# The o projection by seven products: where the sums of its weights and operands are made, and when its operands are loaded

## The chip, the cores and the metric

The kernel runs on one core of one Trainium2 chip. Its engines work side by side: TensorE (PE in the profile, its weight loads PEld), VectorE (DVE), ScalarE (ACT), GpSimd (POOL) and SyncE (SP), which issues most of the transfers (DMA). Each engine takes its instructions in order, and waits for other engines and for transfers by semaphores. The metric is the time of one execution on the chip in microseconds (us), lower is better. Before the change it is 1758.16 us, the median of three runs (1757.42 to 1760.56).

## What is computed

One layer of a hybrid encoder on 1024 positions and 1024 channels in float32: a norm, a projection into many column groups, a convolution module and a bidirectional gated recurrence side by side, a gated merge of the two, an output projection and a feed-forward part. What the change touches are the lines that follow the recurrence, and the layer norm of the convolution module:

```python
a = jax.nn.glu(glu_in, axis=-1)
a = _dwconv_centred(a, dw_w, dw_b)
a = jax.nn.silu(_layernorm(a, ln_w, ln_b))
a = jnp.einsum("bsc,cd->bsd", a, pw_w)
o = _bi_hgrn2(q, v, z_f, z_b, lb[0], lb[1])
...
bmix = (of * jax.nn.silu(og.astype(jnp.float32))).astype(h.dtype)
bmix = jnp.einsum("bse,ed->bsd", bmix, o_w)                      # the o projection
return jax.nn.sigmoid(g_a) * a + jax.nn.sigmoid(g_b) * bmix      # the merge
...
x = x + h @ w_out
```

## The kernel before

**Precision.** A float32 matrix product is made of three passes in a reduced format: each operand is split into a high part (a cast on ACT) and a low part (a subtraction on DVE or POOL; `split`, L126), and `mm3` (L150 to L152) adds high by high, high by low and low by high.

**Seven products.** Large projections are cut into 2 x 2 blocks and made by seven block products instead of eight. For that, sums of blocks of the weights and sums of blocks of the operand are needed. For the o projection the operand is the recurrence's gated output, kept in DRAM as d_bm[head][half] (eight heads of 128 channels, two halves of 512 positions). Blocks are b11 (heads 0 to 3, half 0), b12 (heads 0 to 3, half 1), b21 (heads 4 to 7, half 0) and b22 (heads 4 to 7, half 1). Products 1, 2 and 3 use blocks as they are, products 4 to 7 use sums: 7 is b22 - b12, 5 and 6 and 4 build on it and on b11 and b21. Each product has four columns of output and four slices k of 128 channels.

**Order.** PE's order is written out in the program. Work that must be done beside it is queued by `later(n, f)`: f runs n steps of the stream of products later, and issues its instructions at that place. The other engines' order is made by the framework's scheduler from there, except that an instruction given to `pin` keeps its place in the program. SP's transfers go in its own order; a transfer that waits holds up those behind it.

**The stages, in order of time.**

- *The convolution's norm* (`conv_norm`, L1107 on; about 375 to 470 us, two halves). DVE subtracts the mean (L1124), ACT squares, DVE adds the squares (L1129, three times), PE sums over partitions into the bank ob (L610), DVE and POOL make the reciprocal root (L614, L583, L584). Between these steps PE works on other products. In the same stretch `o_sums` (L1085) loads blocks of the o weights (L1090), adds them on DVE (L1094, four a time, 32 in all) and stores them in d_os (L1095); its start and its additions are set by O_STEP and O_LATE.
- *The scan* (about 600 to 882 us): eight heads one after another, with a stream of other products between; POOL spreads state rows (L1395, S<-D) and makes the root of each head's norm (L583, L584). `scan_outputs` scales the head's output, transposes it (L1484), multiplies by the gate (L1486) and stores d_bm (L1487). `bm_loads` (L1525) reads half 0 back and splits it as operand of products 1 and 2.
- *The o projection* (882.28 to 998.84 us): 28 products of 12 matmuls each, in the order 1 (four columns), 2 (four), 6 (four), then 7 and 4 by turns, 5 (four), 3 (four). Weights come in 14 groups of two products (`o_load`, tag wr, two buffers). `operands` (L1620 on) reads d_bm back, makes the sums (L1635; slices 0 to 2 on POOL, slice 3 on DVE) and splits them. After a product with a finished block, `merge` (L1588) loads a gate from d_gb, multiplies (L1602, L1604), adds the convolution's part by an accumulating transfer on POOL's queue (L1605) and splits the outcome into pages mg. Product 7's outcome is copied from its bank to xq on ACT (L1689) before product 4 adds on to the same bank.
- *The projection by w_out* (998.84 to 1094.26 us), and beside both of these `weight_sums` (L1709): sums of the next layer part's weights, loaded at L1715, added on DVE at L1724 and stored in d_us at L1725.

Of the kernel before, what the change touches and what calls it, by code (L numbers as in the profile page):

```python
# [24 lines left out]
O_LATE, O_STEP = 5, 4  # L25
# [24 lines left out]
def tile_hybrid_encoder(  # L50
# [418 lines left out]
    cp.tile([P, ALIGN // 4 - 8], F32, name="offset")  # L469
# [87 lines left out]
    d_us = [dp.tile([P, 4, ND // 2 * P], F32, name=f"d_us_{n}") for n in range(3)]  # L557
    d_os = [dp.tile([P, 4, ND // 2 * P], F32, name=f"d_os_{n}") for n in range(ND // 2)]
# [526 lines left out]
    def o_sums(n):  # L1085
# [6 lines left out]
        def add():  # L1092
            for a, b in ((0, 1), (1, 2), (2, 0), (3, 2)):
                pin(V.tensor_tensor(t[:, a], t[:, a], t[:, b], op=ALU.add))  # L1094
            nc.sync.dma_start(d_os[p].rearrange("p q (k e) -> p q k e", e=P)[:, :, ks], t)  # L1095

        later(O_LATE, add)
# [116 lines left out]
    none = hp.tile([P, ALIGN // 2], mybir.dt.bfloat16, name="none")[:, :32]  # L1214
# [224 lines left out]
    def scan_outputs(h, kept, Sf, Sb):  # L1439
# [41 lines left out]
        for half in range(2):  # L1481
# [5 lines left out]
            nc.sync.dma_start(d_bm[h][half], bt)  # L1487
            yield
# [34 lines left out]
    b_o = {i: [None] * NK2 for i in range(1, 8)}  # L1523

    def bm_loads():  # L1525
        for h in range(NH - 1):
            t = page(hp, "A", 8)
            nc.sync.dma_start(t, d_bm[h][0])
            behind = last_turned if h < NH - 2 else last_scaled
            with tc.issue_after(behind[0].ins):  # L1530
                b_o[1 + h // NK2][h % NK2] = split(hx(), hx(), t, V)
# [84 lines left out]
    b_pages = {i: [(mg_page(), mg_page()) for _ in range(NK2)] for i in (4, 5)}  # L1616

    def operand(i, k, t):
        pages = b_pages[i][k] if i in b_pages else (hx(), hx())
        b_o[i][k] = split(*pages, t, V)  # L1620

    def operands(k):
        eng = V if k == NK2 - 1 else G
        b11, b12, b22, b21 = [
            h7_page(d_bm[k + h * NK2][half]) for h, half in ((0, 0), (0, 1), (1, 1), (1, 0))
        ]
        if k == NK2 - 1:
            operand(2, k, b21)
        for i, o, a, b, op in (
            (7, b22, b12, b22, ALU.subtract),  # L1630
# [602 lines left out]
```

## Time and profile before

| what | value |
|---|---|
| time, median of three runs | 1758.16 us (1757.42 to 1760.56) |
| the profiled execution | 1759.66 us, span of its instructions 1757.9 us |
| mean clock granted to PE | 0.983 of full speed |
| PE busy in the norm's windows | 6.55 us of 390 to 400, 5.16 us of 450 to 460 |
| o projection | 116.56 us long, PE busy 84.69, DMA share 0.83 |
| projection by w_out | 95.42 us long, PE busy 90.76, DMA share 0.54 |

The page gives busy times of each engine over the whole span. The view of waits names, for each engine, the instruction that waited and what ended the wait. A window lists, for each engine, its busy time and in brackets its instructions, then the clock granted to PE (1.00 is full), the mean share of the DMA engines and GB/s. A row of the timeline has start and length in us, the engine, the line, the operation, the tiles (out<-in), a count where like instructions follow one another, and in square brackets the idle time before it with what ended it. A row of grouped instructions has after the bar the busy us and the mean ns of one, then idle time.

### The profile page before, as it was taken

To read this page: it belongs to the slowest core of one execution; us is meant where nothing else is said; L and a number is where in the kernel's file an instruction comes from. 1 tells how busy PE (TensorE), PEld (TensorE's weight loads), DVE (VectorE), ACT (ScalarE), POOL (GpSimd) and SP (SyncE) were. 2 spreads that over 40 slices of the span, in tenths; PEclk is the share of its full clock that TensorE was granted. 3 is DMA by queue.
4 is the path that set the end of the run, shared out by engine and by line. 5 is a ranking of instruction groups with operands and counts; after the bars stand their busy time and mean duration, and the time that the engine had idled before them with its cause. 6 is when DMAs were issued, how large, how long until landed. Compare 5 with 4: busy or idle time off the path is not lost. (4 is left out here: it accounts for less than half of the span.)

```text
span 1757.9 us, 30563 instructions
## 1 busy us (share of the span) xinstructions
PE 1696.7 (97%) x11671; PEld 1407.7 (80%) x11671; DVE 1303.5 (74%) x1988; ACT 847.6 (48%) x1592; POOL 278.7 (16%) x315
## 2 busy tenths in 40 slices
PE   9999999999899999999957899999999999999998
PEld 6788888887788888888845678888888888888787
DVE  5888898986678888887575556776777777657865
ACT  7454343334477777776433344543443444442434
POOL 2212222100001111111140100322222212000110
PEclk9999999999899999999979999999999999999999
DMA  6888888866663443437679754676777777683752
GB/s 240 289 210 186 199 196 190 206 215 218 219 229 111 126 143 114 155 104 241 219 231 270 177 172 155 177 168 150 168 174 163 166 178 167 201 265 115 209 104 97
DMA packets 348280, 321.64 MB, mean 183 GB/s; under 512 B 18654, under 2 KB 256358, under 8 KB 348134
## 3 DMA queue, kind: packets, MB, share of 16 engines
q1 hardware_dynamic: 298470, 276.69, 49.0%
q0 software_dynamic: 49664, 43.01, 16.6%
q8 instruction: 91, 1.49, 0.3%
q14 instruction: 55, 0.45, 0.1%
HBM read 212.14 MB, written 89.65 MB: 172 GB/s over the span
## 5 line engine op out<-in xcount | busy, mean ns | idle before, releaser
L150 PE MATMUL mm<-hx,wp 128*128 128x512 f32 x976 | 391.1, 401 | 0.6 <-ACT wp L126 0.6
L152 PE MATMUL mm<-hx,wp 128*128 128x512 f32 x976 | 382.0, 391 | 1.3 <-DVE wp L126 1.3
L151 PE MATMUL mm<-hx,wp 128*128 128x512 f32 x976 | 381.3, 391 | 0.6 <-POOL hx L126 0.6
L126 ACT CAST wp<-wr 128x1024 fp32r<-128x1024 f32 (+2 forms) x152 | 153.2, 1008 | 230.2 <-PE mm L151 164.7
L152 PEld LDWEIGHTS mm<-hx,wp 128*128 128x128 f32 x976 | 183.7, 188 | 42.2 <-DVE wp L126 2.6
L126 DVE TENSOR_TENSOR wp<-wr,wp 128x1024 fp32r<-128x1024 f32 (+2 forms) x150 | 176.9, 1179 | 53.3 <-ACT wp L126 53.0
L150 PEld LDWEIGHTS mm<-hx,wp 128*128 128x128 f32 x976 | 183.9, 188 | 38.2 <-ACT wp L126 1.2
L151 PEld LDWEIGHTS mm<-hx,wp 128*128 128x128 f32 x976 | 184.1, 189 | 36.6 <-POOL hx L126 1.1
L1073 DVE SCALAR_TENSOR_TENSOR acc<-gl,v_b,acc 128x1024 f32<-128x1024 f32 x120 | 153.5, 1281 | 1.7
L150 PE MATMUL tr<-hx,wp 128*128 128x512 f32 x200 | 78.3, 392 | 17.5 <-ACT hx L126 17.5
L442 ACT COPY su<-mm 128x512 f32<-128x512 f32 x82 | 47.8, 583 | 87.1 <-PE mm L152 87.0
L1395 POOL DMA_DIRECT2D S<-D x64 | 36.4, 574 | 281.1 <-ACT jk L1462 125.3
L152 PE MATMUL tr<-hx,wp 128*128 128x512 f32 x200 | 78.2, 391 | 1.6 <-DVE wp L126 1.6
L151 PE MATMUL tr<-hx,wp 128*128 128x512 f32 x200 | 78.2, 391 | 1.3 <-DVE hx L126 1.3
L1218 DVE TENSOR_TENSOR qF<-qF,tb 128x512 f32<-128x512 f32 x96 | 65.7, 684 | 9.5 <-ACT A L1252 8.9
L126 ACT CAST wq<-sw 128x1024 fp32r<-128x1024 f32 x41 | 43.2, 1053 | 59.5 <-PE mm L151 29.8
L1218 DVE TENSOR_TENSOR kG<-kG,tb 128x512 f32<-128x512 f32 x96 | 65.7, 686 | 4.0 <-ACT A L1252 2.3
L1812 DVE SCALAR_TENSOR_TENSOR tm<-gp,v_a,tm 128x512 f32<-128x512 f32 x88 | 66.0, 750 | 3.3 <-ACT tm L1810 1.3
L303 POOL DMA_DIRECT2D sw<-in_ffn_w_up_dram x38 | 49.7, 1484 | 117.5 <-DMA sw<-in_ffn_w_up_dram 79.8
L150 PE MATMUL sc<-hy,wq 128*128 128x512 f32 x164 | 64.4, 393 | 0.0
L151 PE MATMUL sc<-hy,wq 128*128 128x512 f32 x164 | 64.3, 392 | 0.0
L152 PE MATMUL sc<-hy,wq 128*128 128x512 f32 x164 | 64.3, 392 | 0.0
(431 smaller groups left out, 3929.4 us busy)
## 6 DMA issues: line engine op xcount, KB each, us to landing
wr<-in_w_in_dram SPq DMA_DIRECT2D x48, 512.0 KB, 5.7
wr<-in_ffn_w_up_dram SPq DMA_DIRECT2D x22, 512.0 KB, 5.3
sw<-in_w_in_dram SPq DMA_DIRECT2D x38, 256.0 KB, 3.1
d_g<-ft SPq DMA_DIRECT2D x38, 256.0 KB, 2.2
sw<-in_ffn_w_up_dram SPq DMA_DIRECT2D x38, 256.0 KB, 4.2
sw<-in_ffn_w_up_dram POOLq DMA_DIRECT2D x38, 256.0 KB, 6.4
wr<-sw POOLq DMA_DIRECT2D x32, 256.0 KB, 3.2
wr<-wr POOLq DMA_DIRECT2D x32, 256.0 KB, 3.3
```

Source lines behind the costliest of these rows:

```text
L126: parts = A.copy(hi, src), eng.tensor_tensor(lo, src, hi.bitcast(F32), op=ALU.subtract)
L150: T.matmul(acc, whi[:, k, :], ahi, start=first, stop=False, skip_group_check=again)
L151: T.matmul(acc, whi[:, k, :], alo, start=False, stop=False, skip_group_check=again)
L152: T.matmul(acc, wlo[:, k, :], ahi, start=False, stop=last, skip_group_check=again)
L303: G.dma_start(o, a, accum_op=ALU.add)
L442: A.copy(t, acc)
L1073: V.scalar_tensor_tensor(acc, g[:, k : k + S], tap(k), acc, op0=ALU.mult, op1=ALU.add)
L1218: return V.tensor_tensor(o, a, b, op=op)
L1395: G.dma_start(S_t[g : g + 32, :, g : g + 32], D_t[g : g + 32])
L1812: V.scalar_tensor_tensor(c, g[:, o + k : o + k + H], vec("fdw", k * NF + j), c, op0=ALU.mult, op1=ALU.add,)
```

## The change

1. In the norm, the loads of the o weights keep their place within a few steps, but the 32 additions are no longer made five steps after the loads: they are handed back as single closures, and run two a step from the step on which the third addition of squares is out.
2. The operand sums of slices 0 to 2 are made in the scan. `combine(k)` starts after the second half of heads 4, 5 and 6 (k = 0, 1, 2): it loads three blocks of d_bm, and a fourth later, into pages ws (three buffers), has POOL add four times (5, 7, 9 and 17 steps later), and stores each sum in a new place in DRAM, d_bt.
3. In the o stage, operands 6, 7, 4 and 5 of slices 0 to 2 are loaded from d_bt and split, dealt over the stage by `later`; slice 3 is still summed on DVE, also dealt. Loads of operand 3 are dealt in a chain. One half of slice 3 of operand 2 is split straight from the tile that holds it, without a reload. Every third weight group goes to a page sw of another pool, so there are three buffers.
4. The additions of `weight_sums` are pinned to the place where the program issues them.

```diff
-O_LATE, O_STEP = 5, 4
...
+    d_bt = {i: scratch(f"d_bt_{i}", ND // 2) for i in (4, 5, 6, 7)}
...
-        def add():
-            for a, b in ((0, 1), (1, 2), (2, 0), (3, 2)):
-                pin(V.tensor_tensor(t[:, a], t[:, a], t[:, b], op=ALU.add))
-            nc.sync.dma_start(d_os[p].rearrange("p q (k e) -> p q k e", e=P)[:, :, ks], t)
-
-        later(O_LATE, add)
+        def add(a, b):
+            pin(V.tensor_tensor(t[:, a], t[:, a], t[:, b], op=ALU.add))
+            if a == 3:
+                nc.sync.dma_start(d_os[p].rearrange("p q (k e) -> p q k e", e=P)[:, :, ks], t)
+
+        return [lambda a=a, b=b: add(a, b) for a, b in ((0, 1), (1, 2), (2, 0), (3, 2))]
...
     for half in range(2):
+        sums = []
         for n in range(half * ND // 2, half * ND // 2 + ND // 2):
-            later(1 + O_STEP * (n % (ND // 2)), lambda n=n: o_sums(n))
-        for pieces in conv_norm(half):
+            later(6 + 2 * (n % 4), lambda n=n: sums.extend(o_sums(n)))
+        for n, pieces in enumerate(conv_norm(half)):
+            if n == 14:
+                for m in range(16):
+                    later(1 + m // 2, lambda m=m: sums[m]())
             s_pairs.fill(pieces)
...
+            if h == NH - 1 and half == 0:
+                b_o[2][NK2 - 1] = split(*b_pages[2][NK2 - 1], bt, V)
+            if half and NK2 <= h < NH - 1:
+                later(2, lambda: combine(h - NK2))
...
+    def combine(k):
+        def raw(src):
+            t = page(hp, "ws", 3)
+            nc.sync.dma_start(t, src)
+            return t
+
+        def keep(i, o, a, b, op=ALU.subtract):
+            G.tensor_tensor(o, a, b, op=op)
+            nc.sync.dma_start(d_bt[i][k], o)
+
+        b12, b22, b11 = [
+            raw(d_bm[k + h * NK2][half]) for h, half in ((0, 1), (1, 1), (0, 0))
+        ]
+        last = []
+        later(5, lambda: keep(7, b22, b12, b22))
+        later(7, lambda: keep(5, b12, b11, b12))
+        later(9, lambda: keep(6, b11, b22, b11))
+        later(12, lambda: last.append(raw(d_bm[k + NK2][0])))
+        later(17, lambda: keep(4, last[0], b11, last[0], ALU.add))
...
+    for k in range(k3):
+        fetched(0, 3 + k, 6, k, d_bt[6][k])
+    raw3 = [h7_page(d_bm[k3][half]) for half in range(2)]
+    later(3, lambda: raw3.extend(h7_page(d_bm[NH - 1][half]) for half in (1, 0)))
...
+    later(6, last_sums)
+    later(17, lambda: operand(5, k3, raw3[1]))
+    later(18, last_fourth)
+    later(19, lambda: operand(7, k3, raw3[2]))
+    for k in range(k3):
+        fetched(9 + k, 6, 7, k, d_bt[7][k])
+        fetched(17 + k, 4, 4, k, d_bt[4][k])
+        fetched(22 + 2 * k, 5, 5, k, d_bt[5][k])
+
+    def third(k):
+        b_pages.setdefault(3, []).append((hx(), hx()))
+        fetched(0, 5, 3, k, d_bm[k + NK2][1])
 
     for k in range(NK2):
-        operands(k)
-
-    for k in range(NK2):
-        later(28 + 2 * k, lambda k=k: operand(3, k, h7_page(d_bm[k + NK2][1])))
+        later(28 + 2 * k, lambda k=k: third(k))
...
-            o_raws[g] = mp.tile([P, 2 * NK2, P], F32, tag="wr", name=nm("wr"), bufs=2)
+            if g % 3 < 2:
+                o_raws[g] = mp.tile([P, 2 * NK2, P], F32, tag="wr", name=nm("wr"), bufs=2)
+            else:
+                o_raws[g] = fw.tile([P, 2 * NK2, P], F32, tag="sw", name=nm("sw"), bufs=1)
...
-                V.tensor_tensor(t, a, b, op=ALU.add)
+                pin(V.tensor_tensor(t, a, b, op=ALU.add))
```

`fetched(at, late, i, k, src)` loads a page, at steps from now, and splits it late steps after that; `last_sums` and `last_fourth` are the four additions of slice 3 on DVE.

The first place is DVE in the second half of the norm, before the change. os are the o weights and their sums, tm the sum of squares, sw and wr weights of other products.

```order
L1094 TENSOR_TENSOR os_4135<-os_4135 128x256 x2
L1124 SCALAR_TENSOR_TENSOR cx_4017<-ob_4161,cx_4017 128x512 x2
L1129 TENSOR_TENSOR tm_4171<-tm_4171,tm_4191 128x512
L836 TENSOR_TENSOR ev_4252<-tr_4177,su_4207 128x512
L1129 TENSOR_TENSOR tm_4171<-tm_4171,tm_4205 128x512
L126 TENSOR_TENSOR wp_4234<-wr_4225,wp_4233 128x1024
L1094 TENSOR_TENSOR os_4185<-os_4185 128x256 x3
L299 TENSOR_TENSOR sw_4227<-sw_4227,sw_4230 128x1024
L1094 TENSOR_TENSOR os_4185<-os_4185 128x256
L299 TENSOR_TENSOR wr_4225<-wr_4225,sw_4227 128x512
L1129 TENSOR_TENSOR tm_4171<-tm_4171,tm_4216 128x512
```

The same place on DVE in the changed kernel (its lines are shifted by a few: L1093 is L1094 above, L298 is L299, L125 is L126).

```order
L125 TENSOR_TENSOR wp_4071<-wr_4050,wp_4070 128x1024
L1129 TENSOR_TENSOR tm_4182<-tm_4182,tm_4197 128x512
L836 TENSOR_TENSOR ev_4253<-tr_4188,su_4208 128x512
L298 TENSOR_TENSOR sw_4228<-sw_4228,sw_4231 128x1024
L125 TENSOR_TENSOR wp_4235<-wr_4226,wp_4234 128x1024
L1129 TENSOR_TENSOR tm_4182<-tm_4182,tm_4206 128x512
L298 TENSOR_TENSOR wr_4226<-wr_4226,sw_4228 128x512
L1129 TENSOR_TENSOR tm_4182<-tm_4182,tm_4217 128x512
L298 TENSOR_TENSOR wr_4226<-wr_4226 128x512
L614 COPY r_667_4284<-ob_4279 128x4
L125 TENSOR_TENSOR rp_4289<-r_667_4284,rp_4288 128x4
L1093 TENSOR_TENSOR os_4108<-os_4108 128x256 x4
```

The sums of os have moved behind the last square and L614; the second square now stands behind the addition into sw as well, which the third one alone did before.

The second place is POOL at the end of the scan, before. S<-D are the state rows, ors the norm of the last head, h the operands' blocks.

```order
L1395 DMA S_10165<-D_9774 32x4x32 x4
L583 TENSOR_SCALAR ors_10408<-oss_10407 128x8
L584 TENSOR_TENSOR ors_10408<-ors_10408,mhalf 128x8
L1635 TENSOR_TENSOR h_1732_10670<-h_1731_10668,h_1732_10670 128x512
L1635 TENSOR_TENSOR h_1731_10668<-h_1730_10666,h_1731_10668 128x512
```

And in the changed kernel, where ws are the pages of `combine(2)`:

```order
L1399 DMA S_10208<-D_9811 32x4x32 x4
L1552 TENSOR_TENSOR ws_10427<-ws_10425,ws_10427 128x512
L1552 TENSOR_TENSOR ws_10425<-ws_10429,ws_10425 128x512
L1552 TENSOR_TENSOR ws_10429<-ws_10427,ws_10429 128x512
L1552 TENSOR_TENSOR ws_10687<-ws_10429,ws_10687 128x512
L583 TENSOR_SCALAR ors_10461<-oss_10460 128x8
L584 TENSOR_TENSOR ors_10461<-ors_10461,mhalf 128x8
```

Four of the twelve additions now stand ahead of the last head's norm; the two other batches of four stand likewise behind two earlier groups of S<-D.

The third place is ACT in the o stage, before, around the first copy of product 7 into xq. hx and mg are high parts of operands and of merged columns, wp of weights.

```order
L126 CAST wp_10986<-wr_10904 128x1024
L126 CAST mg_10951<-tm_10944 128x512
L126 CAST wp_11017<-wr_10959 128x1024
L1689 COPY xq_11037<-ob_11024 128x512
L126 CAST wp_11068<-wr_10990 128x1024
L1601 COPY x_1820_11059<-ob_11024 128x512
```

And in the changed kernel (L125 is L126, L1748 is L1689, L1633 is L1601); the two casts ahead of the copy read operand 3.

```order
L125 CAST mg_10735<-h_1816_11011 128x512
L125 CAST mg_10739<-h_1820_11040 128x512
L125 CAST wp_11060<-wr_10977 128x1024
L125 CAST hx_11098<-h_1830_11100 128x512
L125 CAST hx_11135<-h_1841_11137 128x512
L1748 COPY xq_11082<-ob_11067 128x512
L125 CAST hx_11155<-h_1845_11157 128x512
L125 CAST hx_11192<-h_1856_11194 128x512
L125 CAST wp_11113<-sw_11023 128x1024
```

The casts of operand 3 and of operands 7, 4 and 5, which stood at the start of the stage or far from the copy, now stand directly ahead of it and behind it.

More of the change, by code (lines that the diff above doesn't have):

```diff
@@ L1614, in h7_page @@
         return t
-    b_pages = {i: [(mg_page(), mg_page()) for _ in range(NK2)] for i in (4, 5)}
+    for i in (4, 5):
+        b_pages[i] = [(mg_page(), mg_page()) for _ in range(NK2)]
     def operand(i, k, t):
[L1619 to L1630, printed above, removed]
-            (5, b12, b11, b12, ALU.subtract),
-            (6, b11, b22, b11, ALU.subtract),
-            (4, b21, b11, b21, ALU.add),
-        ):
-            eng.tensor_tensor(o, a, b, op=op)
-            operand(i, k, o)
+        b_o[i][k] = split(*b_pages[i][k], t, V)
```

29 lines of the change are left out of this document (26 added, 3 removed).

## The prediction

> **What bounds the kernel now.** I read the busy shares on the page first, then TensorE's waits, then windows over the stages that the change touches.
>
> ```profile
> span 1757.9 us, 30563 instructions
> PE 1696.7 (97%) x11671; PEld 1407.7 (80%) x11671; DVE 1303.5 (74%) x1988; ACT 847.6 (48%) x1592; POOL 278.7 (16%) x315
> ```
>
> TensorE (PE) is the bound, and its order of work is not changed, so a gain can only come from its idle time and from the time in which its clock is down. The view of waits, for PE, says where it idles (total, times, longest):
>
> ```profile
> PE tr L150 <- ACT hx L126: 17.5, 1, 17.5
> PE ob L610 <- DVE tm L1129: 8.3, 2, 4.8
> PE tr L150 <- ACT xq L1689: 8.2, 2, 7.6
> ```
>
> The first and third lie in the o projection, the second in the two halves of the convolution's norm. The windows show them with the clock beside them (length, then busy time and count of each engine, then the granted clock, DMA share, GB/s; the last two rows are the o stage and the stage of w_out behind it):
>
> ```profile
> 390.00:400.00 10.00, 6.55 (x30) 5.24 (x29) 8.94 (x18) 3.87 (x6) 0.00 (x0) 0.93 0.49 161
> 400.00:410.00 10.00, 10.00 (x36) 8.22 (x37) 2.68 (x4) 4.76 (x12) 1.23 (x2) 0.72 0.44 137
> 450.00:460.00 10.00, 5.16 (x24) 4.04 (x22) 7.17 (x12) 1.93 (x3) 0.00 (x0) 0.84 0.91 290
> 460.00:470.00 10.00, 10.00 (x34) 8.22 (x34) 1.90 (x5) 4.16 (x11) 1.21 (x2) 0.65 0.10 36
> 882.28:998.84 116.56, 84.69 (x339) 66.28 (x338) 73.67 (x91) 39.06 (x58) 29.99 (x25) 0.87 0.83 235
> 998.84:1094.26 95.42, 90.76 (x384) 72.80 (x383) 51.73 (x73) 39.93 (x60) 2.60 (x3) 0.96 0.54 161
> ```
>
> One o product is 12 matmuls, the stage 28 x 12 = 336. The timeline shows one line's matmul again after three:
>
> ```profile
> 866.37 0.39 PE L151 MATMUL mm<-hx,wp 128*128 128x512 f32 x1
> ...
> 867.05 0.39 PE L151 MATMUL mm<-hx,wp 128*128 128x512 f32 x1
> ```
>
> So 0.227 us each, and 336 x 0.227 = 76.3 us for the stage against its 116.6: 40.3 us are lost there, 31.9 as idle time and the rest by a slow clock. That is the most this stage can give.
>
> **Part 1: the weights' sums behind the norm's squares.** In the norm, PE waits at L610 for the third addition of squares, L1129, on VectorE (DVE), which takes its work in order:
>
> ```profile
> 389.79 1.80 DVE L1094 TENSOR_TENSOR os<-os 128x256 f32<-128x256 f32 x4
> ...
> 393.89 0.68 DVE L1129 TENSOR_TENSOR tm<-tm,tm 128x512 f32<-128x512 f32 x1
> ...
> 451.26 0.68 DVE L1129 TENSOR_TENSOR tm<-tm,tm 128x512 f32<-128x512 f32 x1
> ...
> 456.66 1.23 DVE L299 TENSOR_TENSOR sw<-sw,sw 128x1024 f32<-128x1024 f32 x1 [2.33 <-DMA sw<-in_w_in_dram]
> ...
> 458.74 0.68 DVE L1129 TENSOR_TENSOR tm<-tm,tm 128x512 f32<-128x512 f32 x1
> ```
>
> Half 0: eight sums (3.4 us) stand in the 11 us ahead of its squares. With them behind, the third addition ends some 3.4 us earlier, about when PE comes to it (PE idles 10 - 6.55 = 3.45 us). So the wait goes, and with it the slow clock: 10 x 0.07 + 10 x 0.28 = 3.5, less 0.3 that fell into the idle time. Gain 3.45 + 3.2 = 6.7 us.
>
> Half 1: PE idles 10 - 5.16 = 4.8 and loses about 3.7 to the clock (1.6 + 3.5 of the two windows, less half of the 3 idle us that were slow). But here the sums are not what ends last: the last square stands behind the addition at 456.66, which waited for a load, and in the changed order a weight split and two squares stand behind that load. SP issued the load late because two stores of sums stood ahead of it in its queue:
>
> ```profile
> 447.75 1.46 SPq L377 DMA_DIRECT2D sw<-in_w_in_dram  x1
> 449.31 0.52 SPq L1095 DMA_DIRECT2D d_os<-os  x1
> 449.88 0.63 SPq L380 DMA_DIRECT2D sw<-in_w_in_dram  x1
> ```
>
> Those stores go behind it. I put the load some 3 us earlier, at 453.3 (estimate; 452 to 454.5), and the work after it at 4.2 us, by the rows' spacing (1.14 + 1.14 + 3 x 0.6). PE then waits 3 of its 5 us. Gain 2.0 and half of the clock's loss, 1.8: **3.8** (0 to 8.5). Part 1 together: **10.5** (6.7 to 15.2). The sums that move behind fall where DVE has room: 2.68 and 1.90 us busy of 10 in the windows that follow the two waits.
>
> What the clock costs hangs on how long the rest of a wait may be. The rows around the second wait:
>
> ```profile
> 454.50:456.50 2.00, 0.13 (x1) 0.00 (x0) 0.00 (x0) 0.00 (x0) 0.00 (x0) 1.00 1.12 359
> 456.50:459.50 3.00, 0.03 (x1) 0.03 (x1) 2.84 (x5) 0.00 (x0) 0.00 (x0) 0.54 0.52 160
> 459.50:467.00 7.50, 7.50 (x22) 6.24 (x23) 0.85 (x3) 3.10 (x10) 1.21 (x2) 0.50 0.19 68
> ```
>
> The clock halved some 2 us after PE stopped and stayed there for 7.5 us of full work. The Trainium skill (TensorE: Matmul & The Clock Gate, "What's actually happening") puts the drop after about 3.4 us without work and the return after about 3.4 us of it. By that the slow clock would cost 1.7 us a wait, a wait of 3 us would cost none, and part 1 would sum to 3.45 + 1.7 + 2.0 + 1.7 = 8.9; the trace, with an earlier drop and a return twice as long, does not agree, so I keep the rows' sum.
>
> **Part 2: the sums of operands by GpSimd in the scan.** Before, twelve additions stood at the start of the o stage on GpSimd (POOL), and DVE's splits beside them:
>
> ```profile
> L1635 POOL TENSOR_TENSOR h<-h,h 128x512 f32<-128x512 f32 x12 | 18.6, 1560 | 22.5 <-issue 21.8
> ...
> L126 DVE TENSOR_TENSOR hx<-h,hx 128x512 fp32r<-128x512 f32 x11 | 12.3, 1119 | 4.7 <-ACT hx L126 4.0
> ...
> L1635 DVE TENSOR_TENSOR h<-h,h 128x512 f32<-128x512 f32 x4 | 2.7, 685 | 0.0
> ```
>
> and one of those splits in the timeline:
>
> ```profile
> 907.48 1.53 DVE L126 TENSOR_TENSOR hx<-h,hx 128x512 fp32r<-128x512 f32 x1
> ```
>
> A DVE addition of this size takes 0.69 alone and 1.53 beside one of POOL: 12 x 0.84 = 10.1 us of DVE, which now fall in the scan in three batches of 3.4.
>
> ```profile
> 786.01 2.18 POOL L1395 DMA_DIRECT2D S<-D  x4 [16.50 <-ACT jk L1462]
> ...
> 807.99 2.50 POOL L1395 DMA_DIRECT2D S<-D  x4 [12.42 <-DVE qF L1218]
> 828.85 2.18 POOL L1395 DMA_DIRECT2D S<-D  x4 [18.36 <-ACT jk L1462]
> ...
> 868.75 0.20 POOL L583 TENSOR_SCALAR ors<-oss 128x8 f32<-128x8 f32 x1 [18.20 <-ACT jk L1462]
> ```
>
> and the windows over the batches:
>
> ```profile
> 800.00:820.00 20.00, 20.00 (x338) 16.87 (x337) 19.70 (x43) 12.77 (x26) 2.49 (x4) 1.00 0.65 230
> 820.00:840.00 20.00, 20.00 (x353) 17.71 (x351) 12.21 (x29) 11.37 (x37) 4.03 (x6) 1.00 0.63 192
> ```
>
> POOL is free between its groups for the 6 us of a batch. DVE is not, from 800 to 820, but has 7.8 us to itself in the next 20, so a lag of 3.4 is made up unless PE was just behind. PE is busy throughout, and no row says how far ahead of it DVE works. From nothing to all 10.1; the row of 20.00 in both windows speaks for near nothing: **1.5 lost**. The Trainium skill (SBUF — State Buffer, "Practical consequences") has a rule against this move: a DVE operation with two operands in SBUF and a GpSimd one that reads it exclude each other for a whole instruction. By it DVE could lose up to 12 x 1.56 = 18.7 us rather than 10.1; the rows above (1.53 is about a wait plus 0.69) agree with a lock, but DVE's loss is what they measure, and I keep it.
>
> SP also carries 24 more transfers here. Each of the twelve stores of a sum waits in SP's queue for POOL, and behind it stand gate stores, d_ga loads and weight loads. That is a rival below; in the forecast it is within the 1.5.
>
> The third batch stands directly ahead of the norm's L583 at 868.75, which the scan's last head waits for, and its fourth sum needs a load issued late. One addition and part of a wait: **2.4 lost** (0 to 4).
>
> **Part 3: the o stage.** With the sums ready, operand 6 is loaded and split while products 1 and 2 run (8 x 12 x 0.227 = 21.8 us), and the wait of 17.5 goes. A transfer's price, and the landing times, from the view of DMA over the stage:
>
> ```profile
> q1 hardware_dynamic: 22337, 24.19, 64.9%
> q0 software_dynamic: 1701, 3.11, 17.7%
> ...
> h<-d_bm SPq DMA_DIRECT2D x20, 256.0 KB, 4.9
> ...
> tm<-d_a POOLq DMA_DIRECT2D x7, 256.0 KB, 5.1
> ```
>
> So 0.82 us for 256 KB (64.9% of 116.56 over 92 such transfers), and 82.6% of 116.56 = 96 us of DMA in the stage. The stage keeps its 20 operand loads; the weights' sums for the next layer leave it with about 20 transfers (16 us), so 80 us stay: it cannot be much shorter than 80.
>
> New waits take the place of the old one. I walked the changed order of ACT, DVE and SP with these durations (splits 0.69 and 1.22, casts 0.6 and 1.05, landing 4.9 after issue, accumulation 0.85 + 5.1). (a) The third group's weight split stands on DVE behind the last sums, which reload what the last head stored; with the reload at 892.4, three sums at 0.6 and 1.4 for a cast and the split, it ends at 895.6, while PE wants it after four products, at 882.3 + 4 x 2.72 = 893.2: 2.4. (b) The seventh group's split stands behind those of merged gates in the same way: 2.3. (c) The copy of product 7 of column 0 into xq, without which product 4 may not accumulate in that bank, stands on ACT behind casts of the first two third operands. Product 7 ends at 882.3 + 13 x 2.72 + 4.7 = 922.4; the loads are issued near 921.9, once DVE has freed their pages, land 4.9 later, and with 0.9 for two casts and 0.6 the copy ends at 928.2: 5.8, and 3.0 for the clock, as after the waits above. (d) For columns 2 and 3 a copy stands behind the cast of a merged gate, which comes 0.59 + 2 x 0.69 + 0.85 + 5.1 = 7.9 after its product; PE has two products, 5.4, to do meanwhile. So it is already:
>
> ```profile
> 961.77 0.62 ACT L126 CAST mg<-tm 128x512 fp32r<-128x512 f32 x1 [9.64 <-DMA tm<-d_a]
> ...
> 962.78 0.59 ACT L1689 COPY xq<-tr 128x512 f32<-128x512 f32 x1
> ```
>
> The wait of 7.6 above came from there; it stays as 2.6 + 2.8. (e) One at the end, 3.0 (2 to 5). Sum 21.9, against 40.3 before: stage 98.2, **gain 18.4** (8 to 32).
>
> **Part 4: w_out.** It takes the twelve additions and the transfers that left the o stage. DMA share is 0.54 there and DVE busy 51.7 of 95.4, so they are covered; **1.0 lost** (4 lost to 2 gained); without the cover it would be their 12 x 0.69 = 8.2.
>
> **Sum.** 10.5 - 1.5 - 2.4 + 18.4 - 1.0 = 24.0 us. From the profiled execution's 1759.7: 1735.7. That execution stood 1.5 above the median of 1758.2, within the spread of the runs, so I predict **1735**, with 1727 to 1743 as the forecast's own range.
>
> **Rivals.** *Filled (0.20):* the waits (c) to (e) mostly vanish because loads land earlier than I walked. For: PE needs 76.3 and DMA 80; against: the chain from product 7 to 4 is one of ACT's order. Ten us of loss left: gain 30.3, time 1724 (1714 to 1727).
>
> *In-order waits grow (0.20):* the DMA share of 0.83 shows a queue; if the third loads or accumulations land 9 us later, the loss is 31 and the gain 9: 1745 (1743 to 1753).
>
> *The change doesn't do what it says (0.07):* the first wait only moves to operand 6 because its last sum is late. The last load is issued near 886, lands 4.9 later, and product 6 starts at 904, so about 9 us would have to be missing. Price 18.4: 1754.
>
> *Slower (0.08):* SP parked behind the sums. If POOL reaches each batch only with its next group (786.01, 807.99, 828.85: 21 us apart), every load behind the stores is 21 us late; DVE's slack of 7.8 in a group leaves 13 us of stall, three times: 39, and 1735.7 + 37.5 = 1773. It decides from (24 + 1.5) / 3 = 8.5 us a batch. Against: POOL's idle time ahead of each group is 12 to 18 us, and a batch needs 6.
>
> **How the numbers follow.** Forecast 0.45. Leaving out the slower case, most of the one that does nothing and the lower end of the filled one, the range is 1716 to 1752. About 0.2% (3.5 us) is what a measurement here can tell from no change. Faster: 0.45 + 0.20 + 0.20 + 0.03 = 0.88; the same 0.05; slower 0.07.
>
> **What would show it.** Right: no PE wait at L610 in half 0 and one of about 3 us in half 1; no wait of 17 us in the o stage, but three or four of 2 to 6 us at L150, the copies of xq at L1689 named for most; POOL's additions between its groups in the scan, with PE still busy 20.00 of 20 there. Wrong: PE idle in the scan behind d_ga or weights, a DMA share near 1.0 with PE waiting through the o stage, or idle time in w_out behind the sums moved there.

## The result and the profile after

The changed kernel takes **1743.16 us** (median of four runs, 1740.00 to 1746.08) against 1758.84 (1757.42 to 1760.56) before it on the same chip: a ratio of 0.991 (95% interval 0.989 to 0.993), 15.7 us or 0.9% faster. The forecast was 1735; its own range, 1727 to 1743, is missed by 0.2, the wide range, 1716 to 1752, holds the result.

The page, in the lines that answer to those of before:

```profile
span 1741.4 us, 30600 instructions
...
PE 1696.2 (97%) x11671; PEld 1408.4 (81%) x11671; DVE 1304.5 (75%) x1988; ACT 845.4 (49%) x1592; POOL 277.9 (16%) x315
```

The engines do the same work; the span is 16.5 us shorter. The view of waits for PE (engine, tile, line, what released it; us in total, times, longest; lines of the changed kernel up to some L550 are numbered one below those of before, later ones mostly the same up to L1150, and those behind some above):

```profile
PE ob L149 <- ACT xq L1748: 7.3, 2, 6.4
PE mm L149 <- ACT mg L125: 4.4, 3, 2.5
PE mm L149 <- ACT wp L125: 3.3, 1, 3.3
PE ob L610 <- DVE tm L1129: 2.8, 1, 2.8
PE tr L149 <- ACT wp L125: 2.6, 1, 2.6
...
PE ob L1461 <- DVE Sb L1520: 2.1, 1, 2.1
```

The wait of 17.5 us is gone, and so is one of the two at L610. In their place stand waits of 2 to 6 us: 2.6 and 6.4 in the o stage, and two at the end of the scan, where none of before was above 0.6: L149 behind a weight cast (3.3) and L1461 behind Sb (2.1).

What the 17.5 us stood for is in the timeline of the kernel before. The bank is tr, product 2's, so PE waited for the last slice of operand 2, whose cast (912.36) stood on ACT behind twelve casts of operand sums, each of them held by POOL's addition:

```profile
913.03 0.80 PE L150 MATMUL tr<-hx,wp 128*128 128x512 f32 x1 [17.52 <-ACT hx L126]
```

```profile
911.84 0.62 ACT L126 CAST mg<-h 128x512 fp32r<-128x512 f32 x1 [1.05 <-POOL h L1635]
912.36 0.61 ACT L126 CAST hx<-h 128x512 fp32r<-128x512 f32 x1
```

The change takes this away twice: the sums are made in the scan, and that slice of operand 2 is split straight from its tile. No run here has one without the other, so how much of the 17.5 us each of them would have given alone is open.

Windows (length, then busy us and count of each engine, the granted clock, DMA share, GB/s): the two halves of the norm, the end of the scan, the long wait in the o stage and what follows it, the o stage and the stage of w_out.

```profile
390.00:400.00 10.00, 10.00 (x49) 8.39 (x48) 6.71 (x14) 3.76 (x8) 1.44 (x2) 1.00 0.41 131
440.00:450.00 10.00, 7.21 (x32) 5.63 (x30) 5.44 (x8) 2.82 (x5) 0.00 (x0) 1.00 0.72 227
450.00:460.00 10.00, 9.96 (x34) 8.14 (x35) 4.69 (x12) 4.15 (x11) 1.20 (x2) 0.66 0.16 52
855.00:860.00 5.00, 2.89 (x20) 2.44 (x19) 5.00 (x5) 2.20 (x9) 4.31 (x3) 1.00 0.79 267
860.00:865.00 5.00, 5.00 (x26) 4.77 (x25) 0.82 (x2) 1.10 (x4) 0.00 (x0) 0.66 0.77 226
865.00:875.00 10.00, 6.73 (x28) 5.19 (x27) 2.08 (x3) 4.04 (x16) 3.14 (x3) 0.94 0.72 231
...
927.40:934.40 7.00, 0.59 (x4) 0.16 (x2) 6.05 (x10) 6.31 (x11) 0.00 (x0) 0.82 0.71 228
934.40:942.00 7.60, 7.60 (x24) 5.80 (x24) 3.75 (x5) 2.77 (x4) 0.00 (x0) 0.72 0.79 244
...
884.55:981.90 97.35, 83.65 (x338) 65.57 (x337) 56.28 (x78) 37.84 (x57) 11.20 (x13) 0.93 0.81 222
981.90:1077.27 95.37, 90.51 (x385) 72.92 (x384) 59.22 (x85) 40.03 (x60) 2.56 (x3) 0.96 0.72 222
```

The first half of the norm runs without a gap and at full clock; the second keeps a wait of 2.8 us and a slow clock behind it. The o stage has gone from 116.56 to 97.35 us. But it begins at 884.55, **later** than before (882.28), although the norm had put the program some 10 us ahead.

Since both kernels issue the same 11671 matmuls in the same order, the start of each can be compared with that of the same matmul before. The difference, us, gained (-) or lost (+) in each stage, for the changed kernel and for the kernels of the experiments (one profiled execution each; the borders, in times of the kernel before, are 300, 470, 848, 882.28, 998.84 and 1094.26; the last column also holds what differs ahead of the first border and behind the last; joined's execution, at 1735.12, is the slowest of its four):

| kernel | norm | scan to 848 | end of scan | o stage | w_out | all, at 1750 us |
|---|---|---|---|---|---|---|
| changed | -9.7 | +2.2 | **+9.9** | -19.0 | -0.1 | -16.5 |
| conv_only | -11.4 | 0.0 | 0.0 | -1.1 | -0.3 | -11.8 |
| no_adds | -10.0 | -0.2 | 0.0 | -15.9 | +0.7 | -24.3 |
| end_fourth | -11.8 | +2.1 | +1.5 | -16.7 | +0.9 | -23.7 |
| end_all | -11.0 | +2.3 | +1.8 | -18.3 | -0.4 | -25.3 |
| third_behind | -11.5 | +2.2 | +10.8 | -19.4 | -1.3 | -19.3 |
| mg_behind | -10.0 | +3.5 | +10.8 | -24.6 | -0.6 | -20.8 |
| both_behind | -10.2 | +2.2 | +9.9 | -28.0 | +1.1 | -24.0 |
| w3 | -12.0 | +2.1 | +10.7 | -25.1 | -0.5 | -23.7 |
| unpinned | -12.2 | +3.0 | +11.6 | -7.4 | -0.2 | -4.8 |
| joined | -8.6 | +3.2 | +5.5 | -25.8 | -0.4 | -24.6 |
| joined_w3 | -9.8 | +3.8 | +5.1 | -27.5 | +0.1 | -27.9 |
| joined_all | -11.0 | +3.2 | +4.5 | -25.0 | -0.5 | -28.5 |

The program up to the scan is the same in all rows, so the norm's column (8.6 to 12.2) also shows how far one execution differs from another: some 2 us each way; the wait left in the second half was 2.0 to 3.7 us in these executions.

Where did the end of the scan lose 9.9 us? POOL's row of time:

```profile
840.76 2.24 POOL L1399 DMA_DIRECT2D S<-D  x4 [10.68 <-DVE kG L1222]
854.52 4.95 POOL L1552 TENSOR_TENSOR ws<-ws,ws 128x512 f32<-128x512 f32 x3 [11.52 <-DMA ws<-d_bm]
868.71 1.28 POOL L1552 TENSOR_TENSOR ws<-ws,ws 128x512 f32<-128x512 f32 x1 [9.24 <-DMA ws<-d_bm]
870.08 0.20 POOL L583 TENSOR_SCALAR ors<-oss 128x8 f32<-128x8 f32 x1
870.36 1.66 POOL L584 TENSOR_TENSOR ors<-ors,mhalf 128x8 f32<-128x8 f32 x1
```

The fourth sum stood at the head of POOL's queue for 9.24 us, waiting for its load, with the last head's root behind it. And DVE's and ACT's rows beside them:

```profile
846.05 0.69 DVE L1184 TENSOR_TENSOR ev<-mm,ev 128x512 f32<-128x512 f32 x1 [4.85 <-DMA ev<-d_ga]
...
854.69 1.76 DVE L125 TENSOR_TENSOR hx<-A,hx 128x512 fp32r<-128x512 f32 x1
856.37 1.38 DVE L1520 SCALAR_TENSOR_TENSOR Sb<-Sb,Tt 128x128 f32<-128x128 f32 x1
...
858.27 1.34 DVE L1520 SCALAR_TENSOR_TENSOR Sb<-Sb,Tt 128x128 f32<-128x128 f32 x1
...
872.06 1.28 ACT L1480 ACTIVATE tm<-tm,ors 128x128 f32<-128x128 f32 x4 [5.90 <-POOL ors L584]
873.24 0.60 ACT L125 CAST wp<-wr 128x512 fp32r<-128x512 f32 x1
```

Beside the three additions DVE's split took 1.76 in place of 0.68 and its state updates 1.38 and 1.34 in place of 0.34, just where PE waited for them (L1461). Before that, at 846.05, DVE had stood 4.85 us for a load of d_ga (1.5 ahead of the same updates in the kernel before); by the matmuls' lead this had already taken 2.1 us of what DVE was ahead, and the three stretched operations took 3.4 more. Then ACT stood for 5.9 us behind the root, with the weight cast that PE needed queued behind it (3.3 at L149). The matmuls' differences within this stretch are +1.0 at 846 us (PE behind the same DVE operation), +4.0 from 857 to 865 (2.4 us of gap, the rest clock at 0.66) and +4.8 at 870 (3.7 us of gap, then clock at 0.77).

### The profile page after: what moved, and what is told of

It is laid out like the page before. It is cut to its first block, busy times and chain, and to the rows that moved or that the text cites. A ratio compares the mean times of both kernels' runs of the same rounds, so it can differ in the third digit from the quotient of the medians.

```text
span 1741.4 us, 30600 instructions
## 1 busy us (share of the span) xinstructions
PE 1696.2 (97%) x11671; PEld 1408.4 (81%) x11671; DVE 1304.5 (75%) x1988; ACT 845.4 (49%) x1592; POOL 277.9 (16%) x315
## 3 DMA queue, kind: packets, MB, share of 16 engines
q0 software_dynamic: 49664, 43.01, 16.7%
## 5 line engine op out<-in xcount | busy, mean ns | idle before, releaser
L149 PE MATMUL mm<-hx,wp 128*128 128x512 f32 x976 | 390.9, 401 | 3.3 <-ACT wp L125 3.3
L125 ACT CAST wp<-wr 128x1024 fp32r<-128x1024 f32 (+2 forms) x148 | 149.0, 1006 | 208.9 <-PE mm L150 159.9
L149 PEld LDWEIGHTS mm<-hx,wp 128*128 128x128 f32 x976 | 183.9, 188 | 40.7 <-ACT wp L125 3.9
L125 DVE TENSOR_TENSOR wp<-wr,wp 128x1024 fp32r<-128x1024 f32 (+2 forms) x146 | 171.9, 1177 | 45.4 <-ACT wp L125 36.0
L149 PE MATMUL tr<-hx,wp 128*128 128x512 f32 x200 | 79.1, 395 | 2.6 <-ACT wp L125 2.6
L125 ACT CAST wq<-sw 128x1024 fp32r<-128x1024 f32 x41 | 43.2, 1054 | 61.9 <-PE mm L150 34.8
L149 PE MATMUL sc<-hy,wq 128*128 128x512 f32 x164 | 64.5, 393 | 0.0
```

Source lines behind the costliest of these rows:

```text
L125: parts = A.copy(hi, src), eng.tensor_tensor(lo, src, hi.bitcast(F32), op=ALU.subtract)
L149: T.matmul(acc, whi[:, k, :], ahi, start=first, stop=False, skip_group_check=again)
```

## Experiments

### Part 1 alone

Edit, on the kernel before: the two hunks of the change in `o_sums` and in the loop over `conv_norm`, nothing else.

> The kernel before with part 1 of the change alone (loads and additions of the o weights moved behind the norm's squares). Matmul by matmul, the changed kernel's lead over the one before is 9.7 us at the end of the norm, and stays there up to the scan. If part 1 is worth what that shows, this kernel is 9.7 us faster than the one before: about 1749, with a wait at L610 of some 2.8 us left in half 1 and none in half 0, and an o stage of 116 us as before. Rival: the 32 additions moved later cost DVE in the scan, or the o stage starts at another phase of its queues and gives a part back; then less than 8 us are left at the end.

1748.78 us (median of four, 1747.82 to 1751.18), ratio 0.9935 (0.992 to 0.995): 11.4 us faster by the ratio. The gain of the norm stays whole through the scan (0.0 there), and the o stage has its old wait. Part 1 is worth what the matmuls' lead shows, and it costs PE nothing later in the scan. It gave three quarters of what the whole change gives.

### The additions of combine, without them

Edit, on the changed kernel:

```diff
         def keep(i, o, a, b, op=ALU.subtract):
-            G.tensor_tensor(o, a, b, op=op)
             nc.sync.dma_start(d_bt[i][k], o)
```

This kernel leaves the sums out and stores the raw blocks in their place, so its output is not the layer's; it serves for the time alone.

> The changed kernel with the twelve additions of combine left out on GpSimd: the raw blocks are stored in d_bt in place of the sums, with the same 24 transfers. The changed kernel loses 12.2 us against the one before between the start of the scan's second half and the o stage: 2.3 up to 848 us, 1.0 + 4.0 up to 866, 4.8 at the last head's root. Theory 1 (GpSimd's additions: VectorE slowed beside them, the root behind the fourth): nearly all 12 come back, about 1731. Theory 2 (the 24 transfers in SP's queue and on the DMA engines): only the 4.8 at the root come back, about 1738, and TensorE still waits near 857.

1735.34 us (one run). The loss in the scan is gone altogether: -0.2 up to 848 and 0.0 after it, with the same 24 transfers. So all 12 us come from the twelve additions on POOL (19 us of its time), and none from the transfers themselves as long as nothing on SP waits for a sum. The run does not part the additions' ways to PE: beside DVE and the root there are the stores, for which SP stood 21.9 us behind POOL's sums between 750 and 885 us in the changed kernel, in nine waits of at most 4.6. DVE's longest wait for d_ga shortly ahead of its updates of Sb is 1.7 here, 1.5 in the kernel before and 2.4 in conv_only; in the eleven kernels with the additions it is 2.9 to 6.7. The time is not 1731 since the o stage gives 3 us back (15.9 gained in place of 19.0): its waits behind the third group and behind xq are 3.7 and 7.5 in place of 2.6 and 6.4.

### The fourth sum behind the last root

Edit, on the changed kernel (`end_root` holds the last head's L584; `tc.issue_after` queues an instruction behind another of its engine):

```diff
-        later(17, lambda: keep(4, last[0], b11, last[0], ALU.add))
+        def fourth():
+            keep(4, last[0], b11, last[0], ALU.add)
+
+        def behind_root():
+            with tc.issue_after(end_root[0].ins):
+                fourth()
+
+        later(17, fourth if k < NK2 - 2 else behind_root)
```

> The changed kernel with one addition moved: the fourth sum of combine(2) stands on GpSimd directly behind the last head's root (L583, L584 in the changed kernel) and not ahead of it. Theory 1: the root waited for that addition, the addition for its load (landed near 868.6, while the squares were done at 866.2); the weight cast behind the scaling on ScalarE then let TensorE wait 3.3 us and cost 1 of clock. So 4.8 us come back: 1738.4. Rival: the weight cast is late by itself (its load, or ScalarE's order), then less than 1.5 come back. Theory 1 also says that the wait near 857 stays.

1736.91 us (median of four, 1735.51 to 1740.10), ratio to before 0.987 (0.9854 to 0.9887). The wait at the root is gone, as theory 1 had it. The timeline of POOL in this kernel (L584 and L585 are the root here):

```profile
848.98 4.75 POOL L1556 TENSOR_TENSOR ws<-ws,ws 128x512 f32<-128x512 f32 x3 [8.08 <-DMA ws<-d_bm]
859.75 0.20 POOL L584 TENSOR_SCALAR ors<-oss 128x8 f32<-128x8 f32 x1 [6.02 <-ACT jk L1468]
860.03 1.66 POOL L585 TENSOR_TENSOR ors<-ors,mhalf 128x8 f32<-128x8 f32 x1
863.51 1.29 POOL L1556 TENSOR_TENSOR ws<-ws,ws 128x512 f32<-128x512 f32 x1 [1.82 <-DMA ws<-d_bm]
```

The root now waits for its squares (L1468) alone. Against the theory, the wait near 857 went as well, though its three additions had not been moved: their loads landed earlier here (8.08 us of waiting in place of 11.52), and DVE had waited 2.9 us for d_ga in place of 4.85, so the additions met DVE where it was further ahead of PE. Three of its updates of Sb were stretched all the same (1.38, 0.82 and 1.38), but PE waited only 0.4 us for them. What the additions cost depends on landing times.

### All four behind the root

Edit: `keep(7)`, `keep(5)` and `keep(6)` of `combine(2)` likewise behind `end_root`.

> The changed kernel with all four additions of combine(2) behind the last head's root. Theory 1: beside the 4.8 us of the root, the wait of 2.4 us near 857 (VectorE's L1520 at 1.38 for two beside GpSimd's additions) and the slow clock after it go as well, 4.0 together: 8.8 less than the changed kernel, 1734.4. Rivals: the wait near 857 is that of a d_ga load, then it stays and the time is 1738; or the sums are now late for product 6, then TensorE waits in the o stage near 904 and a part is given back there.

1735.37 us (median of four, 1733.95 to 1737.67), ratio 0.9858 (0.9843 to 0.9872). The end of the scan costs 1.8; the expected 8.8 less than the changed kernel is 7.8. DVE's wait for d_ga is 5.3 here and no update of Sb is stretched, and PE does not wait for Sb: as far as these executions show, the wait of 2.1 in the changed kernel took both. But a new wait of 2.0 us stands at the first product of the o stage (the table counts it there): the fourth store waits on SP for POOL, and a d_ga load behind it is late, as joined_all shows below. Between this and end_fourth the intervals overlap, so the three additions' own 4 us are not settled by this pair.

### What held the copy into xq

Three kernels on the changed one. The first puts the splits of operand 3 behind the first copy, the second issues the splits of the gates merged after products 1 and 2 fourteen steps later, the third does both.

```diff
+    copied = []
+
     def operand(i, k, t):
+        if i == 3:
+            with tc.issue_after(copied[0].ins):
+                b_o[i][k] = split(*b_pages[i][k], t, V)
+            return
         b_o[i][k] = split(*b_pages[i][k], t, V)
...
-                    A.copy(seventh[p], acc)
+                    copied.append(A.copy(seventh[p], acc))
...
-        mg[i][half] = split(mg_page(), mg_page(), t, V)
+        def parts():
+            mg[i][half] = split(mg_page(), mg_page(), t, V)
+
+        if e + half == 0:
+            later(MG_LATE, parts)
+        else:
+            parts()
```

ACT in the changed kernel, ahead of the copy that PE waited for from 927.5:

```profile
927.70 0.62 ACT L125 CAST mg<-tm 128x512 fp32r<-128x512 f32 x1 [3.74 <-DMA tm<-d_a]
928.23 3.21 ACT L125 CAST mg<-h 128x512 fp32r<-128x512 f32 x6
931.35 1.04 ACT L125 CAST wp<-wr 128x1024 fp32r<-128x1024 f32 x1
932.29 0.61 ACT L125 CAST hx<-h 128x512 fp32r<-128x512 f32 x1
933.13 0.62 ACT L125 CAST hx<-h 128x512 fp32r<-128x512 f32 x1 [0.22 <-DMA h<-d_bm]
933.65 0.58 ACT L1748 COPY xq<-ob 128x512 f32<-128x512 f32 x1
```

At its head a cast waits for an accumulating transfer, and everything behind it follows at once; the casts of operand 3, which the prediction blamed, are the last 1.4 us.

> The changed kernel with ScalarE's casts of operand 3 (and VectorE's subtractions behind them) queued behind the first copy of product 7 into xq. Theory of the prediction, step (c): these casts, late by their loads, held the copy; then the wait of 6.4 us at L149 behind xq goes almost wholly, with its clock, and some 7 us come back: about 1736. Rival, from the trace of the changed kernel: at the head of ScalarE's queue stood the cast of a merged gate until 927.7, when its accumulating transfer landed, then six casts of operands 7, 4 and 5 (3.2 us) and one of weights; the casts of operand 3 are the last 1.4 us. Then the wait is still about 5 and the time about 1741.5.

1740.33 us (one run). The wait is 4.5 in place of 6.4, and the o stage as long as in the changed kernel within 0.4 us. The rival holds.

> The changed kernel with the splits of the four merged gates of products 1 and 2 issued fourteen steps later, so that the last of them stands behind the copies into xq on ScalarE. The casts of operand 3 stay ahead of the first copy. Theory from the trace (ScalarE's queue stands behind an accumulating transfer): the wait of 6.4 falls to 2.5 or less, and 4 to 6 us come back: about 1738. Theory of the prediction, step (c) (the late loads of operand 3): the wait stays near 6, 1743.

1738.91 us (one run). The wait is 2.0; the o stage gains 24.6 in place of 19.0.

> The two edits of third_behind and mg_behind together. By either theory nothing late is then queued ahead of the first copy into xq: the wait of 6.4 and its slow clock go, 7 to 8 us come back, about 1735.5. Rival: the o stage is bound by its transfers (DMA share 0.81); then TensorE waits elsewhere in the stage, for weights or operands, and less than 3 us come back.

1736.56 us (median of four, 1733.82 to 1738.23), ratio 0.9876 (0.9847 to 0.9905): 6.6 below the changed kernel's median, and in its profile the o stage gains 28.0 in place of 19.0, with the longest wait behind xq at 1.4. So the in-order queue of ACT held the copy, for most of it by the gate's cast.

### The third weight group's load

Edit, on the changed kernel: operand 6's and slice 3's loads three to six steps later, and the last sums three steps later.

```diff
-        fetched(0, 3 + k, 6, k, d_bt[6][k])
-    raw3 = [h7_page(d_bm[k3][half]) for half in range(2)]
+        fetched(4 + k, 4, 6, k, d_bt[6][k])
+    raw3 = []
+    later(3, lambda: raw3.extend(h7_page(d_bm[k3][half]) for half in range(2)))
...
-    later(6, last_sums)
+    later(9, last_sums)
```

> The changed kernel with the loads of operand 6 and of slice 3 issued three to six steps later in the o stage, so that the third weight group's loads stand ahead of them on SP, and its cast ahead of operand 6's casts on ScalarE. Theory: TensorE's first wait in the stage (2.6 us and its tail, 895 to 899) is that of the third weight group's load, which SP issued behind five operand loads; then it goes, 2.5 to 4 us come back in the stage, and nothing new is late, since operand 6 is used some 10 us later. Prediction's step (a): VectorE's split of that group stands behind the last sums; then moving the sums to a later step, which this edit does as well, gives the same, but the trace of the changed kernel would have to show VectorE late, not ScalarE waiting for the load, as it does. Rival: the wait moves on to the fourth group or to product 6, and the stage keeps its length within 1 us.

1735.97 us (one run). The stage gains 25.1 in place of 19.0. ACT in the changed kernel and in this one, where the cast of the third group (from the page sw) stands:

```profile
892.80 0.62 ACT L125 CAST hx<-h 128x512 fp32r<-128x512 f32 x1 [7.51 <-DMA h<-d_bt]
893.71 1.26 ACT L125 CAST hx<-h 128x512 fp32r<-128x512 f32 x2 [0.28 <-DMA h<-d_bt]
897.24 1.04 ACT L125 CAST wp<-sw 128x1024 fp32r<-128x1024 f32 x1 [2.26 <-DMA sw<-in_hgrn_o_w_dram]
```

```profile
892.24 1.05 ACT L125 CAST wp<-sw 128x1024 fp32r<-128x1024 f32 x1 [8.70 <-DMA sw<-in_hgrn_o_w_dram]
```

The wait of 2.6 is gone. That is 6 us of stage for a wait of 2.6 and its slow clock: the rest is the wait behind the first copy into xq, 1.4 here, which this edit was not aimed at (the one behind the third copy grew from 1.2 to 3.0). They hang on when the accumulating transfers land; what shifted those was not tried.

### The pin on the next weights' sums

Edit: `pin(...)` taken off the additions of `weight_sums`.

> The changed kernel without the pin on the additions of weight_sums: VectorE makes them, and SP stores them, some 20 transfers earlier, in the o stage as before. Prediction's part 4 and its floor of 80 us of transfers: the o stage becomes longer by up to 4 us and w_out shorter by up to 1. Rival: the stage's waits are those of single loads and in-order queues, not of the DMA engines' sum; then o stage and w_out change by less than 1 us each.

1754.88 us (one run): 11.7 of the 15.7 us are gone. Its windows (o stage, w_out):

```profile
885.10:994.05 108.95, 88.68 (x338) 68.45 (x337) 62.13 (x88) 37.91 (x57) 10.87 (x13) 0.89 0.88 247
994.05:1089.23 95.18, 89.73 (x384) 72.66 (x383) 53.03 (x75) 39.94 (x60) 2.87 (x4) 0.98 0.56 166
```

The stage is 11.6 us longer than in the changed kernel, w_out as long as there (95.18 against 95.37). DMA work in the stage is 0.88 x 108.95 = 95.9 us, against 0.81 x 97.35 = 78.9: the 17 us that were moved. Idle time of PE is 20.3 against 13.7, and the clock 0.89 against 0.93. Both my 4 us and the rival were too small: this one line carries more than half of the stage's gain of 19. The edit puts twelve additions of DVE (8.2 us) back into the stage along with the transfers, and the run does not part the two. One wait is plainly a transfer's: PE's behind the third copy into xq is 4.5 in place of 1.2, and the cast ahead of that copy waited 4.14 in place of 0.89 for the accumulation into d_a.

### Put together

joined is end_fourth with both_behind; joined_w3 adds w3; joined_all puts all four additions behind the root.

> end_fourth, third_behind and mg_behind together. The root edit gave 8 us at the end of the scan in its run, the two others 9 in the o stage in theirs. If they add up: about 1743.2 - 17 = 1726. Rival: what the stage's start comes earlier, its first loads come late, since they follow the last head's stores; then 2 to 4 are given back there: 1729.

1731.45 us (median of four, 1731.14 to 1735.12), ratio 0.985 (0.9835 to 0.9865): above the expected 1726 and the rival's 1729. At the end of the scan PE waits 2.7 us for a DVE operation that waited 6.7 for d_ga.

> joined with the edit of w3. If the first wait of the stage goes: 3 to 4 us below joined, 1723 to 1725. Rival as for w3: the wait moves on, and it equals joined within 1.5 us.

1730.52 us (median of five, 1727.00 to 1735.00), ratio 0.9839 (0.982 to 0.9858). The stage's first wait is gone, but against joined the difference is within the spread, as the rival had it.

> joined_w3 with all four additions of combine(2) behind the last head's root, as in end_all, in place of the fourth alone. In joined_w3 the end of the scan still cost 5.1 us beside the kernel before (waits of 2.3 near 848 and 2.0 near 861, the latter behind VectorE's Sb beside GpSimd's additions); in end_all it cost 1.8. If the additions make the wait near 861, it goes, and 2 to 3.5 us come back: about 1727.5. Rival: the three additions now land where the o stage's first operands are split, or their stores delay the loads behind them on SP; then the stage gives it back and the time equals joined_w3 within 1.5 us.

1729.55 us (median of five, 1727.48 to 1732.00), ratio 0.9824 (0.981 to 0.9837), the lowest median here, though its interval and joined_w3's overlap; 30.8 us below the kernel before on its chip (1760.37), and 13.6 below the changed kernel's median on another. The wait near 861 went, and a new one came, as the rival said, whose condition (within 1.5 us of joined_w3) the time meets. SP and DVE in this kernel:

```profile
876.72 0.32 SPq L1560 DMA_DIRECT2D d_bt<-ws  x1
877.14 0.38 SPq L1186 DMA_DIRECT2D ev<-d_ga  x1
```

```profile
880.37 0.69 DVE L1187 TENSOR_TENSOR ev<-mm,ev 128x512 f32<-128x512 f32 x1 [4.85 <-DMA ev<-d_ga]
```

The store of the fourth sum waits on SP for POOL, the load of d_ga stands behind it, DVE waits for that load, and PE for DVE (1.9). The parts do not add up: 8 at the scan's end and 9 in the stage were gained apart, by the matmuls, and 11.7 together in joined, by the medians.

## Why the prediction was right, and where it was off

- **The sum** was 24.0 us and the matmuls show 16.5; the wide range held 1743. Of the difference of 7.5, one term carries all, the end of the scan; the others miss by about 1 us or less each and cancel.
- **The norm**: 10.5 expected, 9.7 in the changed kernel's profile, 11.4 timed alone. Half 0 gave 7.4 (6.7 expected), with no wait left; half 1 gave 2.3 (3.8 expected) and keeps a wait of 2.8 (3 expected). Both waits came out as forecast. The half of the clock's loss that I credited in half 1 did not come: 0.66 in the window after it. So the rule of the Trainium skill (TensorE: Matmul & The Clock Gate, "What's actually happening"), by which a wait under 3.4 us costs no clock, did not hold here either.
- **The scan up to 848**: 1.5 expected, 2.2 found; no_adds shows that POOL's additions make it, as the prediction said. Its sign, PE busy 20.00 of 20 there, did not hold: 19.00 to 20.00 in the windows of 20 us from 748 to 848.
- **The end of the scan**: "One addition and part of a wait: 2.4 lost (0 to 4)" was the step that failed; it measured 9.9. The mechanism at L583 was the one named, but the fourth sum's load landed 2.5 us after the squares were done (868.7 against 866.2), the addition came on top, and then the clock: 4.8, above my upper end. The three additions before it I had counted into the scan's 1.5; 4.0 us fell on PE there, and 1.0 at 846 behind d_ga. The timeline of the kernel before had the bound that I did not look up, DVE's last update of Sb and PE's matmul that reads it:

```profile
860.25 0.34 DVE L1512 SCALAR_TENSOR_TENSOR Sb<-Sb,Tt 128x128 f32<-128x128 f32 x1
```

```profile
863.90 0.39 PE L1457 MATMUL ob<-Sb,qF 128*128 128x128 f32 x2
```

  DVE was 3.3 us ahead there, and lost 5.5 against PE (2.1 for d_ga, 3.4 beside the additions), while I had judged by its idle time in windows of 20 us (7.8 of 820 to 840). The Trainium skill's rule that was weighed there (SBUF — State Buffer, "Practical consequences": two such operations of VectorE and GpSimd exclude each other) agrees with 1.38 and 1.34 in place of 0.34, a wait for most of an addition; that it fell on the path was not in the rule but in that lead.
- **The o stage**: 18.4 expected, 19.0 found, and that it is so near is in part luck. The first wait went, as forecast; of the new ones few came as walked. (a) 2.4 at the third group: 2.6, but by its load on SP, not by VectorE behind the last sums (w3). (b) 2.3 at the seventh group: none there. (c) 5.8: 6.4, but by the cast of a merged gate at the head of ACT's queue; the casts of operand 3 are under 2 of it (third_behind against mg_behind). (d) 2.6 + 2.8: 1.2 + 0.9. (e) 3.0: 0.8 in the stage; the waits behind merged gates (4.4) lie in w_out, where 4.1 stood before. PE's idle time in the stage is 13.7 (97.35 less 83.65), where the terms had 18.9, and the rest of its 21.1 above the floor of 76.3, 7.4, is mostly the slow clock, where they had 3.0: waits put too high and the clock too low, which nearly cancel.
- **w_out**: 1.0 lost expected, nothing found. What I missed is the other side: the transfers that left the o stage stood in the sum only as a floor ("so 80 us stay"; 78.9 measured), but by unpinned they and the additions that make them are worth 11.6 us of the stage.
- **The rivals**: "SP parked behind the sums" did not come at its size: POOL stood ahead of each batch for a load, not in a queue of its own. In small it is there: SP's 21.9 us behind the sums, the 1.0 behind d_ga at 846, and the waits of 2.0 and 1.9 at the start of the o stage in end_all and joined_all. How the late load of 846 follows from SP's waits was not traced step by step. "In-order waits grow" had 1743 to 1753 and so touches the measured time, but not by its mechanism: it gave the stage 9 us, and 19.0 were found. "Filled" came near only with the two edits on ACT: a stage of 88.88 in joined_w3, where I had put 86.

## What to carry to other kernels

Before work is put beside or ahead of something on the path, read in the timeline how long before its use by the bound engine the last result is ready: that lead, not an engine's idle share, is what may be spent, and an addition that waits for a load spends the load's landing time as well. In a queue that runs in order, first move what waits for a transfer, then what is long. And transfers that only prepare the next stage can be worth moving out, with the work that makes them, of a stage with a DMA share of 0.88 even where that share is no bound.

## What the runs showed of the hardware

A gap of about 2 us on PE can halve the clock, but does not always. In the changed kernel 2.2 us without work near 858 were followed by a clock of 0.58 over 3.6 us; in joined_w3 gaps of 2.2 and 1.9 us near 848 and 861 were followed by a clock of 1.00:

```profile
857.40:859.60 2.20, 0.16 (x2) 0.00 (x0) 2.20 (x4) 0.85 (x5) 1.99 (x2) 1.00 0.99 322
859.60:863.20 3.60, 3.53 (x18) 3.53 (x19) 1.22 (x3) 0.00 (x0) 0.00 (x0) 0.58 0.62 209
```

```profile
860.40:862.30 1.90, 0.16 (x2) 0.00 (x0) 1.90 (x4) 0.85 (x5) 0.86 (x1) 1.00 0.90 260
862.30:868.00 5.70, 5.67 (x35) 5.08 (x36) 1.86 (x3) 2.20 (x9) 0.64 (x2) 1.00 0.63 193
```

In the fourteen traces kept here, each of the 32 gaps of 3.0 us and more was followed by a mean clock of 0.50 to 0.81 over the next 3.5 us. The longest gap that cost no clock is one of 2.99 us, in w3:

```profile
938.79:941.78 2.99, 0.01 (x1) 0.00 (x1) 1.51 (x3) 2.16 (x5) 0.00 (x0) 1.00 0.55 177
941.78:948.40 6.62, 5.73 (x24) 4.43 (x24) 3.21 (x5) 3.06 (x5) 0.85 (x1) 1.00 0.51 85
```
